# Padded feature rows loaded whole, and each group's score products put one step behind its one-hot products

## The chip, the cores and the metric

The kernel runs on one core of a Trainium2 chip. The metric is the device time of one execution in microseconds (us). Three runs of the kernel before took 2100.96, 2101.25 and 2093.63 us; the median is 2100.96 us.

TensorE (PE) multiplies, VectorE (DVE) and ScalarE (ACT) work element by element, GpSimd (POOL) prepares gathers by index and does a few small operations, and SyncE (SP) issues the plain transfers. Every engine works through its own list of instructions strictly in order; an instruction that waits holds up all that stand behind it on its engine.

## The reference, cut to what matters

The model is one layer: a convolution and a state-space branch, a cross-attention, and a layer of product-key experts (PEER). The change lies in the last part, which for 256 tokens, 8 heads and 16 experts per head computes

```
q = (h @ w_q).reshape(tokens, 8, 2, 64)
s = einsum("thsk,hsnk->thsn", q, sub_keys)      # 128 scores per half
s1, i1 = top_k(s[..., 0, :], 16);  s2, i2 = top_k(s[..., 1, :], 16)
top_s, pos = top_k(all 256 sums of s1 and s2, 16)
idx = i1[...] * 128 + i2[...]                   # of the 16 sums taken
g = softmax(top_s)
act = gelu(einsum("td,tkd->tk", h, u_tab[idx])) # 128 experts per token
out = einsum("tk,tkd->td", g * act, v_tab[idx])
```

`u_tab` and `v_tab` have 16,384 rows of 2048 numbers.

## The kernel before

The tokens are two tiles of 128, tile 0 and tile 1. The scores `h . u` are computed in two parts. Columns 768 to 2047 of each chosen row of `u_tab` are gathered, one row for each of the 128 tokens at a time: POOL issues the gather (L924, into one of five buffers `u`), and DVE forms the dot product with the token (L926, with `hnF`). I call one such pair a dot; there are 256, 128 for each tile. For columns 0 to 767, `dense` multiplies all 16,384 rows with all tokens on PE (`sy`, L972, with `hnT`) and stores the scores in the large tiles `WA` (tile 0) and `WB` (tile 1). Dots and dense products run beside each other.

Then comes the settling: out of the 16,384 dense scores of a token, the 128 wanted ones have to be picked. An index is two numbers of 0 to 127, and a one-hot row of each is made by a small product: `feats` holds five numbers per pick and token (the square of the index in two parts, the index, and two ones), `C` five constants, and their product `d` is 1 - (index - k)^2, which after a Relu is 1 at the index and 0 elsewhere. For a group of four tokens, `extract` makes the two one-hot tiles `E` and `H` in this way (four products `d` at L992 and a Relu on ACT at L994 for each), and at once multiplies the scores by `E` (`y`, L1000 for tile 0 and L1003 for tile 1). `pick` multiplies `H` by `y` on DVE (L1010) and adds up the columns on PE (`more`, L1012). I call the DVE product of `pick` an H product. `LAG` says how many groups later `pick` follows. Each tile has 32 groups.

When tile 0 is picked, `finish` adds the dots and the picked scores, applies the gelu and the gate (`ptc`, `cT`, L907 to L917), and while tile 1 is picked, the weights of tile 0 are spread out into `WA` again: `left` makes the one-hot tiles `dr` and `L` (L1019, L1028), and `build` scales one (`R`, DVE, L1035), multiplies the two on PE (`pw`, L1038) and copies the result (ACT, L1039). After the last dot tile 1 is finished and the last 4 groups of tile 0 and the 32 of tile 1 are built. Only then does the last stage run, a dense product with `v_tab` beside gathers of it (from 1556 us on).

Four things set the order. The list of DVE is written by hand: the program emits a dot, then as many steps of the settling as a pace gives (2.2 steps per dot, a step being a `yield` in `settle`), then the next dot. The lists of the other engines are set by a planner. The settling begins at dot 176 (`SETTLE_AT`). The features lie in `fe_dram` in device memory and are loaded by `load_feats` into memory that is free by then: tile 0's into `hnF`, once the dots of tile 0 are done, and tile 1's into `hnT`, once the dense products are done. `load_feats` first clears its 128 rows on POOL (L934), since the four groups of rows that SP loads (L937) have 20 rows each, 5 for each of four tokens, and are placed 32 rows apart.

Of the kernel before, what the change touches and what calls it, by code (L numbers as in the profile page):

```python
# [9 lines left out]
F32 = mybir.dt.float32  # L10
F32R = mybir.dt.float32r
BF16 = mybir.dt.bfloat16
I32 = mybir.dt.int32
U32 = mybir.dt.uint32
AF = mybir.ActivationFunctionType
# [5 lines left out]
P = 128  # L21
T = 256
NTT = T // P
# [15 lines left out]
NSLOT = PH * TOPK  # L39
# [25 lines left out]
SETTLE_RATE = 2.2  # L65
SETTLE_AT = 176
FEATS_AT = 150
LAG = (2, 1)
DELAY = 16
HOLD = 4  # L70
RAW_BUFS = 4
HI_BUFS = 3
LO_BUFS = 4
FEAT = 5
NROW = 4 * FEAT


@with_exitstack
def trunk(ctx, tc, a, out, dbg=None):
# [12 lines left out]
    ones = consts.tile([P, P], F32, name="ones")  # L92
# [25 lines left out]

    C = consts.tile([P, 4, 4, P], BF16, name="C")
    c_dram = dram.tile([FEAT, P], BF16, name="c_dram")  # L120
    fe_dram = [dram.tile([P, FEAT, 2 * NSLOT], BF16, name=f"fe_dram{tt}") for tt in range(NTT)]

    def load_consts(t, ones):
        ones = ones[:, :2 * NSLOT].bitcast(BF16)
        G.memset(ones, 1.0)
        for d in fe_dram:
            SY.dma_start(d[:, 3:].rearrange("p f x -> p (f x)"), ones)
        rows, one_less_sq = t[0:1, :FEAT * P // 2].bitcast(BF16), t[0:1, 3 * P:4 * P]
        k = iota[0:1, :P]
        G.memset(rows[:, :2 * P], -1.0)  # L130
        G.tensor_scalar(rows[:, 2 * P:3 * P], k, 2.0, None, op0=ALU.mult)
        G.tensor_mul(one_less_sq, k, k)
        G.tensor_scalar(one_less_sq, one_less_sq, -1.0, 1.0, op0=ALU.mult, op1=ALU.add)
        G.tensor_copy(rows[:, 3 * P:4 * P], one_less_sq)
        G.tensor_sub(rows[:, 4 * P:], one_less_sq, rows[:, 3 * P:4 * P])
        SY.dma_start(c_dram.rearrange("f k -> (f k)")[None, :], rows)
        G.memset(C, 0.0)
        for b in range(4):
            for i in range(4):
                p0 = 32 * b + FEAT * i  # L140
                SY.dma_start(C[p0:p0 + FEAT, b, i, :], c_dram)

    wbx = ctx.enter_context(ExitStack())
# [787 lines left out]
    fe_at = [x[:, :NQ * NSLOT // 4].bitcast(BF16).rearrange("p (j s k) -> p j s k", s=2, k=NSLOT) for x in room]  # L931

    def load_feats(tt):
        G.memset(fe_at[tt], 0.0)  # L934
        src = fe_dram[tt].rearrange("(b j i) f x -> b (i f) j x", b=4, i=4)
        for b in range(4):
            SY.dma_start(fe_at[tt][32 * b:32 * b + NROW].rearrange("f j s k -> f j (s k)"), src[b])  # L937

    coef = [consts.tile([P, NSLOT], F32, name=f"coef{tt}") for tt in range(NTT)]
    vidx = [consts.tile([P, NSLOT], I32, name=f"vidx{tt}") for tt in range(NTT)]  # L940
# [40 lines left out]
    def feats(route, g):  # L981
        return fe_at[route.tt][:, g % 8], C[:, g // 8]

    def extract(route, g):
        psq, lr_q = settling_pools
        f, cs = feats(route, g)
        spread = route.tt == 0 and g % 4 > 1
        one = []
        for s, nm in ((1, "E"), (0, "H")):
            d = psq.tile([P, 4, P], F32, name="d")  # L990
            for i in range(4):
                PE.matmul(d[:, i, :], cs[:, i, :], f[:, s, :], start=i == 0, stop=i == 3, skip_group_check=True)  # L992
            one.append(lr_q.tile([P, 4, P], F32, name=nm, tag="R" if spread and nm == "H" else nm))
            S.activation(one[-1], d, AF.Relu)  # L994
        E, H = one
        y = psq.tile([P, 4, P], F32, name="y", tag="dr" if spread else "y")
        for i in range(4):
            t = 4 * g + i
            if route.tt == 0:
                PE.matmul(y[:, i, :], W[0][:, t, :], E[:, i, :], start=i == 0, stop=i == 3, skip_group_check=True)  # L1000
            else:
                for h in range(2):
                    PE.matmul(y[64 * h:64 * h + 64, i, :], by_token[:, h, t, :], E[:, i, :], start=i == 0, stop=i == 3,  # L1003
                              skip_group_check=True)
        return H, y

    def pick(route, g, H, y):
        if g == 0:
            route.more = psu.tile([P, NSLOT], F32, name="more", bufs=1)
        V.tensor_mul(H, H, y)  # L1010
        for i in range(4):
            PE.matmul(route.more[i * NQ:(i + 1) * NQ, :], onecol[:, NQ - g:2 * NQ - g], H[:, i, :], start=g == 0,  # L1012
                      stop=g == NQ - 1)
# [55 lines left out]

    def settle():  # L1070
        groups = P // 4
        held = {}
        for tt in range(NTT):
            lefts = []
            lag = LAG[tt]
            for n in range(groups + lag):
                if n < groups and (tt, n) not in held:
                    held[tt, n] = extract(routes[tt], n)
                    yield
                if n >= lag:  # L1080
                    pick(routes[tt], n - lag, *held[tt, n - lag])
                    yield
                if tt:
                    if n > HOLD:
                        build(routes[0], n - HOLD - 1, *lefts.pop())
                    if n >= HOLD:
                        lefts.append(left(routes[0], n - HOLD))
                    yield
            if tt == 0:
                while tick[0] <= NSLOT:  # L1090
                    yield
                for n in range(2):
                    held[1, n] = extract(routes[1], n)
                yield from routes[0].finish()
            else:
                held_left.append(lefts.pop())
# [157 lines left out]
```

## Time and profile before

| | us |
|---|---|
| median of three runs | 2100.96 |
| profiled execution, its own time | 2093.88 |
| span of its profile | 2092.1 |
| dense products of `u_tab` end, settling starts on PE | 1293.6 |
| first H product of tile 0 starts on DVE | 1320.5 |
| `cT` of tile 0 on DVE | 1388.6 |
| last `y` of tile 1 starts on PE | 1493.1 |
| last dot starts on DVE | 1503.8 |
| last stage starts on ACT and PE | about 1556 |

PE is busy for 94% of the span, DVE for 80%, ACT for 48% and POOL for 38%. The stages follow each other, so what matters is what each stretch waits for; a busy share of the whole span says little of it.

### The profile page before, as it was taken

How to read it: one execution, taken by the hardware profiler on the slowest of the kernel's cores; microseconds unless marked ns; L12 is line 12 of the kernel's file. 1: busy time of each engine (PE TensorE's matmuls, PEld its weight loads, DVE VectorE, ACT ScalarE, POOL GpSimd, SP SyncE). 2: the span in 40 equal slices, each digit the busy share in tenths (PEclk: the TensorE clock that was granted, in tenths of full speed). 3: DMA queues.
4: the chain of work that ended last, by engine and by line, in shares of the span. 5: the costliest groups of instructions: out<-in, count | busy, mean ns of one | idle time of the engine just before them, and what ended most of it. 6: DMA issues, size and time to landing. Idle time of an engine off the chain costs nothing.

```text
span 2092.1 us, 33295 instructions
## 1 busy us (share of the span) xinstructions
PE 1969.4 (94%) x12359; PEld 1689.5 (81%) x12379; DVE 1683.7 (80%) x2757; ACT 998.4 (48%) x1586; POOL 786.6 (38%) x590
## 2 busy tenths in 40 slices
PE   7999999999999999899999998689899999999997
PEld 7888886786899888778888887567677888888886
DVE  6699998995756558999976663988868899899998
ACT  5776665445545444333333323356563444444444
POOL 1111111000000003444446753643217677677775
PEclk9999999999999999999999999899999999999999
DMA  7888788757854567989999996988629999999996
GB/s 233 198 239 210 194 224 224 219 193 216 286 182 159 178 194 278 306 304 332 328 368 398 398 394 220 330 273 265 189 106 317 359 337 339 341 340 341 338 335 231
DMA packets 201428, 570.99 MB, mean 273 GB/s; under 512 B 31266, under 2 KB 37779, under 8 KB 201138
## 3 DMA queue, kind: packets, MB, share of 16 engines
q1 hardware_dynamic: 134130, 306.69, 43.8%
q0 software_dynamic: 67136, 262.18, 37.5%
q8 instruction: 97, 1.59, 0.3%
q14 instruction: 65, 0.53, 0.1%
HBM read 556.34 MB, written 12.45 MB: 272 GB/s over the span
## 4 chain that ended last, share of the span: by engine, by line
PE 56%; DVE 18%; issue 10%; DMA 8%; POOL 6%; ACT 2%; SPq 0%; DVEq 0%; POOLq 0%; ACTq 0%
PE acc L1201 8%; PE acc L1202 8%; PE acc L1200 8%; DVE u L926 5%; POOL u L924 5%; PE mm L202 3%; PE mm L212 3%; PE mm L201 3%; PE mm L203 3%; PE mm L210 3%; PE mm L211 3%; PE pw L1038 3%; PE y L1003 2%; DMA w_lo<-in_w_kv_mem 2%; PE y L1000 2%
## 5 line engine op out<-in xcount | busy, mean ns | idle before, releaser
L926 DVE SCALAR_TENSOR_TENSOR u<-u,hnF 128x1280 f32<-128x1280 f32 x256 | 387.7, 1517 | 110.9 <-DMA u<-in_peer_u,uidx 109.9
L1165 POOL DMA_INDIRECT v<-in_peer_v,vidx x256 | 388.3, 1517 | 187.8 <-DVE accg L1167 82.1
L924 POOL DMA_INDIRECT u<-in_peer_u,uidx x256 | 303.1, 1184 | 316.3 <-DVE u L926 226.0
L972 PE MATMUL sy<-hnT,ut 128*128 128x256 f32 x1536 | 356.0, 384 | 14.1 <-ACT ut L968 14.1
L187 ACT CAST w_hi<-w_raw 128x1024 fp32r<-128x1024 f32 (+2 forms) x228 | 231.2, 1017 | 242.5 <-PE mm L203 114.6
L972 PEld LDWEIGHTS sy<-hnT,ut 128*128 128x128 f32 x1536 | 286.7, 192 | 54.8 <-ACT ut L968 19.4
L192 DVE TENSOR_TENSOR w_lo<-w_raw,w_hi 128x1024 fp32r<-128x1024 f32 (+2 forms) x192 | 226.4, 1181 | 110.3 <-ACT w_hi L187 110.1
L103 ACT CAST vh<-vr 128x1472 fp32r<-128x1472 f32 x128 | 183.1, 1431 | 258.6 <-PE acc L1201 257.1
L1201 PE MATMUL acc<-vh,wl 128*128 128x512 f32 (+1 forms) x768 | 295.9, 385 | 6.1 <-DVE wl L1191 6.1
L1202 PE MATMUL acc<-vl,wh 128*128 128x512 f32 (+1 forms) x768 | 293.9, 385 | 0.8 <-DVE vl L104 0.8
L212 PE MATMUL mm<-aT_hi,w_lo 128*128 128x256 f32 x960 | 273.1, 292 | 15.7 <-DVE w_lo L192 6.6
L210 PE MATMUL mm<-aT_hi,w_hi 128*128 128x256 f32 x960 | 277.9, 292 | 0.7 <-ACT w_hi L187 0.7
L1200 PE MATMUL acc<-vh,wh 128*128 128x512 f32 (+1 forms) x768 | 275.7, 383 | 2.4 <-ACT vh L103 2.4
L211 PE MATMUL mm<-aT_lo,w_hi 128*128 128x256 f32 x960 | 275.3, 289 | 0.0
L104 DVE TENSOR_TENSOR vl<-vr,vh 128x1472 fp32r<-128x1472 f32 x128 | 216.7, 1693 | 42.5 <-ACT vh L103 42.1
L1167 DVE SCALAR_TENSOR_TENSOR accg<-v,coef,accg 128x576 f32<-128x576 f32 x256 | 208.8, 816 | 11.1 <-DMA v<-in_peer_v,vidx 7.1
L212 PEld LDWEIGHTS mm<-aT_hi,w_lo 128*128 128x128 f32 x960 | 184.2, 195 | 22.4 <-DVE w_lo L192 8.0
L210 PEld LDWEIGHTS mm<-aT_hi,w_hi 128*128 128x128 f32 x960 | 186.7, 195 | 6.6 <-issue 3.7
L211 PEld LDWEIGHTS mm<-aT_lo,w_hi 128*128 128x128 f32 x960 | 187.0, 195 | 3.4 <-issue 2.0
L1201 PEld LDWEIGHTS acc<-vh,wl 128*128 128x128 f32 x768 | 144.8, 189 | 36.8 <-DVE wl L1191 6.6
L1200 PEld LDWEIGHTS acc<-vh,wh 128*128 128x128 f32 x768 | 144.6, 188 | 28.4 <-ACT vh L103 2.6
L1202 PEld LDWEIGHTS acc<-vl,wh 128*128 128x128 f32 x768 | 144.8, 189 | 22.9 <-DVE vl L104 1.2
(380 smaller groups left out, 3193.8 us busy)
## 6 DMA issues: line engine op xcount, KB each, us to landing
vr<-in_peer_v SPq DMA_DIRECT2D x128, 736.0 KB
raw<-in_peer_u SPq DMA_DIRECT2D x128, 384.0 KB
w_raw<-in_w_kv_mem SPq DMA_DIRECT2D x64, 512.0 KB
w_raw<-in_w_in SPq DMA_DIRECT2D x48, 512.0 KB
w_raw<-in_w_out SPq DMA_DIRECT2D x32, 512.0 KB
w_raw<-in_w_q_mem SPq DMA_DIRECT2D x32, 512.0 KB
w_raw<-in_w_o_mem SPq DMA_DIRECT2D x32, 512.0 KB
w_lo<-in_w_kv_mem POOLq DMA_DIRECT2D x24, 512.0 KB, 7.8
```

Of the source, the lines that this page charges most:

```text
L187: S.copy(hi, raw)
L192: V.tensor_sub(lo, raw, hi.bitcast(F32))
L210: PE.matmul(o, wh, ah, start=first and cb % 2 == 0, stop=False, skip_group_check=True)
L211: PE.matmul(o, wh, al, start=False, stop=False, skip_group_check=True)
L212: PE.matmul(o, wl, ah, start=False, stop=last and end, skip_group_check=True)
L924: G.indirect_dma_start(out=u, out_offset=None, in_=a["peer_u"].rearrange("e (q c) -> (e q) c", c=GU), in_offset=bass.IndirectOffsetOnAxis( ...
L926: V.scalar_tensor_tensor(u, u, 1.0, hnF[:, self.tt, :], op0=ALU.mult, op1=ALU.mult, accum_out=self.act[:, j:j + 1])
L972: PE.matmul(ps[:, b % 2, :], ut[:, k, :], hnT[:, k, :], start=k == 0 and b % 2 == 0, stop=k == KD - 1 and b % 2 == 1, skip_group_check=True)
L1165: G.indirect_dma_start(out=v, out_offset=None, in_=table, in_offset=bass.IndirectOffsetOnAxis(ap=vidx[tt][:, j:j + 1], axis=0))
L1200: PE.matmul(o, wh[:, tt, :], vh[:, cs_], start=b == 0, stop=False)
L1201: PE.matmul(o, wl[:, tt, :], vh[:, cs_], start=False, stop=False)
L1202: PE.matmul(o, wh[:, tt, :], vl[:, cs_], start=False, stop=b == NB - 1)
```

## The change

1. `fe_dram` has 8 rows per pick instead of 5 (`ROWS`). The three more are zeros, written once at the start of the kernel, beside the ones that are written there already: eight small transfers on SP (L129, L131 of the changed kernel) instead of two. The constants `C` are placed 8 rows apart instead of 5. `load_feats` then loads all 32 rows of each of its four groups, and the clearing on POOL is gone.
2. `extract` is split. `onehots` makes `E` and `H` of a group, and `select` makes `y`. `settle` calls `onehots` for group n and then `select` for group n - 1; `pick` comes one group later than before (`LAG` is (3, 2) instead of (2, 1)). In tile 1, `H` of every third group lies in a part of `hnT` that the features don't use (`spare_h`). The loop over the groups has one step more per tile, and `onehots` no longer has a step of its own.

```diff
-LAG = (2, 1)
+LAG = (3, 2)
...
-NROW = 4 * FEAT
+ROWS = 8
...
-    fe_dram = [dram.tile([P, FEAT, 2 * NSLOT], BF16, name=f"fe_dram{tt}") for tt in range(NTT)]
+    fe_dram = [dram.tile([P, ROWS, 2 * NSLOT], BF16, name=f"fe_dram{tt}") for tt in range(NTT)]
...
-        ones = ones[:, :2 * NSLOT].bitcast(BF16)
-        G.memset(ones, 1.0)
+        fill = ones.bitcast(BF16)
+        n1, n0 = 2 * (FEAT - 3) * NSLOT, 2 * NSLOT
+        G.memset(fill[:, :n1], 1.0)
+        G.memset(fill[:, n1:n1 + n0], 0.0)
         for d in fe_dram:
-            SY.dma_start(d[:, 3:].rearrange("p f x -> p (f x)"), ones)
+            SY.dma_start(d[:, 3:FEAT].rearrange("p f x -> p (f x)"), fill[:, :n1])
+            for r in range(FEAT, ROWS):
+                SY.dma_start(d[:, r], fill[:, n1:n1 + n0])
...
-                p0 = 32 * b + FEAT * i
+                p0 = 32 * b + ROWS * i
...
     def load_feats(tt):
-        G.memset(fe_at[tt], 0.0)
         src = fe_dram[tt].rearrange("(b j i) f x -> b (i f) j x", b=4, i=4)
         for b in range(4):
-            SY.dma_start(fe_at[tt][32 * b:32 * b + NROW].rearrange("f j s k -> f j (s k)"), src[b])
+            SY.dma_start(fe_at[tt][32 * b:32 * b + 32].rearrange("f j s k -> f j (s k)"), src[b])
...
-    def extract(route, g):
+    spare_h = hnT[:, 4:6, :].rearrange("p k (i s) -> p (k i) s", s=P)
+
+    def onehots(route, g):
         psq, lr_q = settling_pools
         f, cs = feats(route, g)
-        spread = route.tt == 0 and g % 4 > 1
         one = []
         for s, nm in ((1, "E"), (0, "H")):
             d = psq.tile([P, 4, P], F32, name="d")
             for i in range(4):
                 PE.matmul(d[:, i, :], cs[:, i, :], f[:, s, :], start=i == 0, stop=i == 3, skip_group_check=True)
-            one.append(lr_q.tile([P, 4, P], F32, name=nm, tag="R" if spread and nm == "H" else nm))
-            S.activation(one[-1], d, AF.Relu)
-        E, H = one
-        y = psq.tile([P, 4, P], F32, name="y", tag="dr" if spread else "y")
+            if nm == "E":
+                x = lr_q.tile([P, 4, P], F32, name="E")
+            elif route.tt and g % 3 == 2:
+                x = spare_h
+            else:
+                x = lr_q.tile([P, 4, P], F32, name="H", tag="R" if route.tt == 0 and g % 4 > 1 else "H")
+            S.activation(x, d, AF.Relu)
+            one.append(x)
+        return one
+
+    def select(route, g, E, H):
+        psq, lr_q = settling_pools
+        y = psq.tile([P, 4, P], F32, name="y", tag="dr" if route.tt == 0 and g % 4 > 1 else "y")
...
-                if n < groups and (tt, n) not in held:
-                    held[tt, n] = extract(routes[tt], n)
-                    yield
+                if n < groups and (tt, n) not in ones_at:
+                    ones_at[tt, n] = onehots(routes[tt], n)
+                if 0 < n <= groups:
+                    held[tt, n - 1] = select(routes[tt], n - 1, *ones_at.pop((tt, n - 1)))
+                yield
                 if n >= lag:
-                    pick(routes[tt], n - lag, *held[tt, n - lag])
+                    pick(routes[tt], n - lag, *held.pop((tt, n - lag)))
                     yield
...
                 for n in range(2):
-                    held[1, n] = extract(routes[1], n)
+                    ones_at[1, n] = onehots(routes[1], n)
```

How the lists move at three places. First, POOL's list from the dense stage to the end of the settling, before:

```order
L856 TENSOR_TENSOR WB<-WB 128x512 x2
L924 DMA u<-in_peer_u,uidx 128x1280 x59
L934 MEMSET hnF 128x2048
L924 DMA u<-in_peer_u,uidx 128x1280 x35
L934 MEMSET hnT 128x2048
L924 DMA u<-in_peer_u,uidx 128x1280 x88
```

and now:

```order
L860 TENSOR_TENSOR WB<-WB 128x512 x2
L928 DMA u<-in_peer_u,uidx 128x1280 x9
L860 TENSOR_TENSOR WB<-WB 128x512 x2
L928 DMA u<-in_peer_u,uidx 128x1280 x182
L1180 DMA v<-in_peer_v,vidx_8418 128x576 x128
```

The clearing of `hnF` and of `hnT` stood among the gathers, the second ahead of the last 88; now the last 182 gathers follow each other with nothing between them. The loads of the features (SP) stay at their places.

Second, PE and ACT in the middle of tile 0's groups (a row of `d` stands for the four of its tile; numbers tell the tiles apart), before:

```order
L992 MATMUL d_12257<-hnF_7777,C_76 128x128
L992 MATMUL d_12264<-hnF_7777,C_76 128x128
L1012 MATMUL more_11822<-H_12191,onecol_8420 32x128 x4
L1000 MATMUL y_12271<-E_12262,WA_8432 128x128 x4
L994 ACTIVATE E_12262<-d_12257 128x512
```

and now:

```order
L996 MATMUL d_12252<-hnF_7784,C_76 128x128
L996 MATMUL d_12259<-hnF_7784,C_76 128x128
L1025 MATMUL more_11844<-H_12156,onecol_8427 32x128 x4
L996 MATMUL d_12279<-hnF_7784,C_76 128x128
L1013 MATMUL y_12293<-E_12257,WA_8439 128x128 x4
L1003 ACTIVATE E_12257<-d_12252 128x512
```

`y` read an `E` whose `d` stood three steps ahead of it on PE, in the same group; now the `d` of the next group's `E` (`d_12279`) stands between as well.

Third, DVE from `cT` of tile 0 on, and at the end of the dots. Before:

```order
L914 TENSOR_TENSOR cT<-cT,gT 128x128
L926 SCALAR_TENSOR_TENSOR u,act<-u,hnF 128x1280
L1010 TENSOR_TENSOR H<-H,y 128x512
...
L1010 TENSOR_TENSOR H<-H,y 128x512
L926 SCALAR_TENSOR_TENSOR u,act<-u,hnF 128x1280
L1035 SCALAR_TENSOR_TENSOR R<-dr,cT 128x512
L926 SCALAR_TENSOR_TENSOR u,act<-u,hnF 128x1280 x3
L1035 SCALAR_TENSOR_TENSOR R<-dr,cT 128x512
L926 SCALAR_TENSOR_TENSOR u,act<-u,hnF 128x1280
L1035 SCALAR_TENSOR_TENSOR R<-dr,cT 128x512
L926 SCALAR_TENSOR_TENSOR u,act<-u,hnF 128x1280
L914 TENSOR_TENSOR cT<-cT,gT 128x128
```

and now:

```order
L918 TENSOR_TENSOR cT<-cT,gT 128x128
L930 SCALAR_TENSOR_TENSOR u,act<-u,hnF 128x1280 x3
L1023 TENSOR_TENSOR H<-H,y 128x512
...
L1023 TENSOR_TENSOR H<-H,y 128x512
L930 SCALAR_TENSOR_TENSOR u,act<-u,hnF 128x1280 x2
L1048 SCALAR_TENSOR_TENSOR R<-dr,cT 128x512
L918 TENSOR_TENSOR cT<-cT,gT 128x128
```

Three dots instead of one stand between `cT` of tile 0 and the first H product of tile 1, and two dots instead of six behind the last H product. Ahead of the first H product of tile 0 stand 179 dots instead of 178. On PE the second `ptc` of tile 0 now stands directly behind the first, where one `d` tile stood between, and `ptc` of tile 1 no longer stands behind two `dr` that wait for the last `R`.

More of the change, by code (lines that the diff above doesn't have):

```diff
@@ L1071, in settle @@
         groups = P // 4
-        held = {}
+        ones_at, held = {}, {}
         for tt in range(NTT):
@@ L1076, in settle @@
             for n in range(groups + lag):
-                if n < groups and (tt, n) not in held:
-                    held[tt, n] = extract(routes[tt], n)
-                    yield
+                if n < groups and (tt, n) not in ones_at:
[3 more added lines that the diff above has]
+                yield
                 if n >= lag:
-                    pick(routes[tt], n - lag, *held[tt, n - lag])
+                    pick(routes[tt], n - lag, *held.pop((tt, n - lag)))
                     yield
                 if tt:
-                    if n > HOLD:
+                    if HOLD < n <= groups:
                         build(routes[0], n - HOLD - 1, *lefts.pop())
-                    if n >= HOLD:
+                    if HOLD <= n <= groups:
                         lefts.append(left(routes[0], n - HOLD))
```

## Prediction

> **What bounds the kernel now.** I read the stretches around the settling first.
>
> ```profile
> core 0: us, PE busy (x) PEld busy (x) DVE busy (x) ACT busy (x) POOL busy (x), PEclk, DMA share, GB/s
> 1245.00:1265.00 20.00, 19.13 (x101) 16.49 (x100) 14.26 (x19) 5.78 (x10) 15.46 (x10) 1.00 1.02 405
> 1275.00:1293.60 18.60, 17.74 (x93) 15.35 (x92) 0.32 (x2) 4.32 (x8) 0.60 (x1) 1.00 0.09 28
> 1293.60:1305.00 11.40, 7.83 (x81) 6.63 (x79) 1.68 (x3) 6.09 (x12) 6.82 (x7) 1.00 0.79 239
> 1305.00:1321.20 16.20, 0.00 (x0) 0.00 (x0) 13.92 (x20) 0.00 (x0) 11.60 (x8) 0.60 0.93 339
> 1391.00:1494.20 103.20, 99.78 (x1201) 75.34 (x1215) 94.33 (x141) 61.75 (x111) 43.68 (x43) 0.95 0.84 265
> 1494.20:1505.40 11.20, 5.84 (x37) 3.02 (x36) 10.95 (x16) 4.81 (x9) 0.94 (x1) 0.88 0.45 148
> 1505.40:1556.00 50.60, 48.19 (x333) 40.83 (x338) 33.28 (x51) 28.53 (x53) 0.00 (x0) 0.92 0.09 27
> 1556.00:2092.00 536.00, 512.85 (x2304) 433.90 (x2304) 475.62 (x658) 242.26 (x406) 388.34 (x256) 0.99 0.92 329
> ```
>
> PE is the bound in nearly every stretch. The exception is 1305 to 1321.2, where it does nothing at all, and just before, from 1275 to 1293.6, DVE and the DMA engines (share 0.09) do nothing. The timeline joins the two holes (start, duration, what, and the idle time ahead of it with its releaser):
>
> ```profile
> 1264.50 1.50 POOL L924 DMA_INDIRECT u<-in_peer_u,uidx  x1 [0.31 <-issue]
> 1293.00 1.80 POOL L934 MEMSET hnT<- 128x2048 bf16 x1 [27.00 <-PE sy L972]
> 1273.81 1.49 DVE L926 SCALAR_TENSOR_TENSOR u<-u,hnF 128x1280 f32<-128x1280 f32 x1 [1.01 <-DMA u<-in_peer_u,uidx]
> 1300.58 1.49 DVE L926 SCALAR_TENSOR_TENSOR u<-u,hnF 128x1280 f32<-128x1280 f32 x1 [25.27 <-DMA u<-in_peer_u,uidx]
> 1319.10 1.49 DVE L926 SCALAR_TENSOR_TENSOR u<-u,hnF 128x1280 f32<-128x1280 f32 x1 [0.27 <-DMA u<-in_peer_u,uidx]
> 1320.52 0.68 DVE L1010 TENSOR_TENSOR H<-H,y 128x512 f32<-128x512 f32 x1
> 1321.25 0.65 PE L1012 MATMUL more<-H,onecol 128*32 128x128 f32 x8 [16.26 <-DVE H L1010]
> ```
>
> The clearing of `hnT` reaches the head of POOL's list at 1266.0 and waits 27.0 us, until the last dense product has read `hnT`. The gathers queue behind it, DVE has no rows for 25.27 us, and ten dots that stand ahead of the first H product in DVE's list are done only afterwards, from 1300.58 to 1320.5. PE, four groups ahead, waits 16.26 us for that product.
>
> **The change, term by term,** against the profiled execution (2093.88 us, span 2092.1).
>
> *Term 1, the stall.* With no clearing the gathers go on at 1266. Eleven dots now stand ahead of the first H product. Their pace is about 2.1 us: 19 records (two for each dot) in 20 us in the first row above, beside the loads of `raw`, and (1319.10 - 1300.58)/9 = 2.06 without them. The last dot in hand ends at 1275.3, so the eleven end at 1275.3 + 11 x 2.1 = 1298.4. PE needs the first H product only after the fourth `y`, which in the trace starts at 1301.36:
>
> ```profile
> 1301.36 1.16 PE L1000 MATMUL y<-E,WA 128*128 128x128 f32 x8 [0.52 <-ACT E L994]
> DMA to landing us min/median/max: 4.5/7.5/12.8
> ```
>
> That is 1302.5, some 4 us later, so the whole 16.26 us goes. With all five buffers at the slowest landing a dot takes 12.8/5 = 2.56 us and the eleven end at 1303.5: 1 us is left over. Bounds 15.2 to 16.3; I take 16.3. The dots advanced use DMA engines that stand still now, and the last loads of `raw` were issued by 1274, so the dense products don't wait longer.
>
> *Term 2, the cold start.* After the hole PE runs slowly:
>
> ```profile
> 1321.84 2.08 PE L1000 MATMUL y<-E,WA 128*128 128x128 f32 x8
> 1326.73 1.16 PE L1000 MATMUL y<-E,WA 128*128 128x128 f32 x8
> ```
>
> One `y` costs 0.92 us more, at a granted clock of 0.60 in the stretch before; with the small products around it I take 1.5, bounds 0.9 to 2. [...]
>
> *Term 3, E before y.* The steady pattern of tile 0, and the waits of PE from 1293.6 to 1383:
>
> ```profile
> 1328.86 1.16 PE L1000 MATMUL y<-E,WA 128*128 128x128 f32 x8 [0.17 <-ACT E L994]
> 1329.85 0.61 PE L992 MATMUL d<-hnF,C 128*128 128x128 bf16 x8
> 1330.39 0.43 PE L1012 MATMUL more<-H,onecol 128*32 128x128 f32 x8
> 1330.99 1.16 PE L1000 MATMUL y<-E,WA 128*128 128x128 f32 x8 [0.17 <-ACT E L994]
> PE y L1000 <- ACT E L994: 4.8, 19, 0.8
> ```
>
> A group takes 2.13 us, of which 0.17 is the Relu of its own `E`. With another group's `d` between, it goes: 4.8 us less the first wait (0.8), which stays. I take 4.0, bounds 2 to 4.8. What then limits? DVE:
>
> ```profile
> 1343.86 1.48 DVE L926 SCALAR_TENSOR_TENSOR u<-u,hnF 128x1280 f32<-128x1280 f32 x1
> 1345.27 0.68 DVE L1010 TENSOR_TENSOR H<-H,y 128x512 f32<-128x512 f32 x1
> 1345.87 1.48 DVE L926 SCALAR_TENSOR_TENSOR u<-u,hnF 128x1280 f32<-128x1280 f32 x1
> ```
>
> A dot holds it for 1.41 us and an H product for 0.60. Tile 0's 32 products with the 29 dots among them take 32 x 0.60 + 29 x 1.41 = 60.1 us, from 1298.4 to 1358.5. The next fence shows DVE idle for 5.31 us ahead of `cT` at 1388.6, after the products and a last dot, so they end near 1382 now. DVE comes some 23 us earlier, the three terms give PE 21.8, and they fit.
>
> *Term 4, from tile 0 to tile 1: a loss.*
>
> ```profile
> 1388.61 0.29 DVE L914 TENSOR_TENSOR cT<-cT,gT 128x128 f32<-128x128 f32 x1 [5.31 <-ACT cT L911]
> 1390.97 0.66 PE L1012 MATMUL more<-H,onecol 128*32 128x128 f32 x8 [1.45 <-DVE H L1010]
> 1391.56 1.98 PE L1003 MATMUL y<-E,WB 128*64 128x128 f32 x16
> ```
>
> Now `more` of tile 1 starts 2.4 us after `cT`. With three dots between, it is 0.3 + 3 x 1.41 + 0.6 = 5.1, and PE, strictly in order, has nothing ahead of that `more` but the second `ptc`; behind it stand the `y` and every `d` of tile 1. That is 2.8 us lost; bounds 1 to 5, since one group more is in flight; I take 3. The restart there is slow already (`y` 1.98 us) and stays so.
>
> *Term 5, tile 1.* PE is busy for 99.78 of 103.2 us from 1391 on; the same products remain. At most 3.4 can be gained, at least 0; I take 1.
>
> *Term 6, the last dots.*
>
> ```profile
> 1493.14 1.09 PE L1003 MATMUL y<-E,WB 128*64 128x128 f32 x16 [0.17 <-ACT E L994]
> 1503.81 1.48 DVE L926 SCALAR_TENSOR_TENSOR u<-u,hnF 128x1280 f32<-128x1280 f32 x1
> 1505.45 0.77 PE L909 MATMUL ptc<-ident,act 128*128 128x128 f32 x2 [0.92 <-DVE u L926]
> ```
>
> From the last `y` to `ptc` pass 12.3 us, in which DVE does six dots and three `R` (6 x 1.41 + 3 x 0.60 = 10.3) after its last H product. Two dots and one `R` are left (3.4), and `ptc` stands ahead of the `dr` that waits for the last `R`. PE's own work between (5.84 busy in the row 1494.2 to 1505.4, and the Relus that it waits for) takes about 8, so 4 us go; bounds 0 to 6.9. Behind `ptc` the 50.6 us of building and the 536 us of the last stage stand as they are and move as a block.
>
> *Term 7, the start.* Six more small writes stand in SP's list among the first weights.
>
> ```profile
> 30.59 0.89 SPq L127 DMA_DIRECT2D fe_dram<-ones  x2
> 35.51 0.30 POOL L130 MEMSET crow<- 1x256 bf16 x1 [8.33 <-DMA fe_dram<-ones]
> 45.00:50.00 5.00, 5.00 (x44) 5.00 (x43) 1.66 (x2) 2.10 (x2) 0.00 (x0) 1.00 0.73 211
> ```
>
> At 0.45 us each they hold SP for 2.7 us; POOL's `crow`, and the write of the constants that SP waits for, come as much later. PE is fully busy there, and three weight loads instead of two now stand ahead of that wait. Bounds 0 to 2.7 lost; I take 0.5.
>
> *Nothing* I give the fuller load of the features: 128 rows instead of 80, 0.5 MB, which for tile 1 is first read some 60 us after its issue; if that cover were gone it would cost under 2 us. The first clearing (of `hnF`) held POOL for less than 2 us and nothing waited.
>
> The sum: 16.3 + 1.5 + 4 - 3 + 1 + 4 - 0.5 = **23.3 us** less, 2070.6 us for an execution like the profiled one. The median of the runs shown lies 7.1 us above that execution, and I can't tell at which level the changed kernel's median will fall, 2070.6 or 2077.7; I put it at **2073**. The bounds of the terms added up as independent (about 5 us either way) and the two levels give 2064 to 2083 for this case.
>
> **The rivals.**
>
> *The advanced dots run slowly* (0.15). Dense loads and gathers shared 405 GB/s, and if the eleven dots took 3.3 us each they would end at 1311.6; PE would still wait 9 us, and the gain be 14: 2080 to 2087. Against it speaks that nothing else loads after the last `raw`.
>
> *Gathers shut out by dots* (0.03). On POOL the settling's gathers read:
>
> ```profile
> L924 POOL DMA_INDIRECT u<-in_peer_u,uidx x74 | 79.7, 1077 | 94.5 <-DVE u L926 89.9 <-issue 4.3 <-DVE H L1010 0.3
> ```
>
> If a gather could not be issued while a dot runs, one dot would cost 1.49 + 1.08 + 0.3 = 2.87 us, the eleven would end at 1306.9, and 4.4 us of term 1 would remain: 2075 to 2082. [...] The trace disagrees: dots follow each other every 2.01 us with an H product between (1343.86 and 1345.87).
>
> *Slower: features and spare H share `hnT`* (0.05). Every third group of tile 1 writes its `H` into the tile from which PE reads the features. If PE's next `d` had to wait for the H product in it, ten groups would each lose a wait. It decides from 23.3/10 = 2.3 us per wait; at a whole group's time, 101.6/29 = 3.5 us between the `y` at 1391.56 and 1493.14, it costs 35, and the time is 2105 to 2113. Against it: the `more` of that `H` waits for the same H product and stands ahead of those `d` on PE.
>
> *No change* (0.06). The gathers meet another wait up to 1293, and the second part gives back in term 4 what it gains in terms 3 and 6: 2092 to 2101. For it speaks only that the dots read `hnF` too, whose first half tile 0's features fill; but that load is issued near 1195.
>
> **How the numbers follow.** The forecast has 0.71, the rivals 0.15, 0.03, 0.05 and 0.06. A measurement of this kernel tells about 0.5% from no change. Against 2101, faster by over 0.5% means below 2090.5: the forecast, the locked gathers and most of the first rival, 0.87. Within 0.5%: 0.08. Slower: 0.05. The range, 2061 to 2088, holds the forecast and most of the slow dots.
>
> **What would show it.** In the changed profile no clearing stands on POOL and no wait of 25 us on DVE; DVE works between 1275 and 1293; the first H product starts near 1298 and PE's first `more` waits for nothing (term 1); few `y` of tile 0 wait for `E` and a group takes 1.96 us (term 3); a hole of some 5 us stands behind `cT`, which comes near 1366 (term 4); the last `y` starts near 1472 and `ptc` 8 us later (terms 5 and 6); the last stage keeps its 536 us. A first H product after 1303, or a PE wait for an H product among tile 1's features, would make me wrong.

## The result, and the profile after

The changed kernel took **2064.7 us** (median of four runs, 2061.8 to 2068.76) against 2098.55 us for the kernel before (four runs). The ratio is 0.9843, with a 95% interval of 0.9815 to 0.987, so about 33 us less. The prediction was 2073 us with a range of 2061 to 2088. The direction and the range held, and the median lies 8 us under the number. The profiled execution took 2064.74 us, with a span of 2063.0. One run each of two kernels below, 2630.97 and 2443.26 us at a mean granted clock of 0.69 and 0.75, was slow and is left out of their medians.

Both holes of the stage around 1300 us are gone. The stretches of the changed kernel (columns as in the prediction):

```profile
core 0: us, PE busy (x) PEld busy (x) DVE busy (x) ACT busy (x) POOL busy (x), PEclk, DMA share, GB/s
1245.00:1265.00 20.00, 19.13 (x103) 16.57 (x102) 13.50 (x18) 6.32 (x12) 15.12 (x9) 1.00 1.02 411
1275.00:1293.60 18.60, 17.74 (x94) 15.42 (x93) 13.06 (x17) 4.53 (x9) 12.35 (x9) 1.00 1.01 398
1293.60:1305.00 11.40, 10.32 (x75) 9.11 (x73) 2.70 (x6) 5.14 (x11) 3.29 (x3) 1.00 0.91 286
1305.00:1321.00 16.00, 15.26 (x194) 12.89 (x193) 15.51 (x23) 9.24 (x17) 6.56 (x7) 1.00 0.73 216
1360.00:1380.00 20.00, 13.50 (x167) 9.25 (x168) 14.46 (x22) 8.03 (x16) 9.27 (x9) 0.84 0.68 238
```

From 1275 to 1293.6 DVE worked for 0.32 us and now works for 13.06; the DMA share there goes from 0.09 to 1.01. From 1305 to 1321 PE goes from nothing to 15.26 of 16 us. One hole is left, in the stretch around `cT`.

To see where the time went, I read from each trace when a few landmarks start, and subtract. "Change" and "before" stand twice because both kernels were profiled a second time. All rows are us.

| stage | before | before, again | padding alone | split alone | change | change, again |
|---|---|---|---|---|---|---|
| start to the first `d` of the settling | 1293.6 | 1300.5 | 1302.5 | 1289.6 | 1301.3 | 1296.6 |
| to the first H product | 26.9 | 27.1 | 2.7 | 27.7 | 2.8 | 2.8 |
| to the last H product of tile 0 | 60.7 | 60.4 | 67.5 | 58.1 | 58.7 | 58.9 |
| to the first H product of tile 1 | 9.0 | 9.0 | 7.3 | 10.5 | 12.1 | 12.1 |
| to the last `y` | 103.7 | 103.5 | 103.7 | 103.8 | 103.6 | 104.1 |
| to `ptc` of tile 1 | 11.8 | 11.9 | 11.9 | 5.3 | 5.3 | 5.3 |
| to the last copy of `pw` | 50.0 | 49.9 | 50.7 | 47.8 | 47.8 | 50.3 |
| to the eighth cast `vh` of the last stage | 35.6 | 35.4 | 28.5 | 28.5 | 28.8 | 28.9 |
| to the end of the span | 500.7 | 500.7 | 502.9 | 502.9 | 502.6 | 502.6 |

With the means of the two profiles of each kernel, the change gives 25.9 us up to the last H product of tile 0, loses 3.1 ahead of tile 1, gives 6.5 after the last `y`, some 0.9 in the building, 6.7 on entering the last stage, and loses 1.9 at the very end and 1.9 ahead of the settling. That sums up to 33 us. The 0.9, the 6.7 and the two losses of 1.9 had no place in the prediction. The loss ahead of the settling is smaller than the difference between two profiles of one kernel (1293.6 and 1300.5 us).

**The stall is gone as forecast.** The timeline of the changed kernel at the places that the prediction quoted:

```profile
1285.91 2.24 POOL L928 DMA_INDIRECT u<-in_peer_u,uidx  x1 [2.19 <-DVE u L930]
1274.75 1.54 DVE L930 SCALAR_TENSOR_TENSOR u<-u,hnF 128x1280 f32<-128x1280 f32 x1 [1.09 <-DMA u<-in_peer_u,uidx]
1293.96 1.49 DVE L930 SCALAR_TENSOR_TENSOR u<-u,hnF 128x1280 f32<-128x1280 f32 x1
1304.09 0.69 DVE L1023 TENSOR_TENSOR H<-H,y 128x512 f32<-128x512 f32 x1 [8.63 <-ACT E L1003]
1309.68 0.42 PE L1025 MATMUL more<-H,onecol 128*32 128x128 f32 x8
1310.03 1.16 PE L1013 MATMUL y<-E,WA 128*128 128x128 f32 x8
```

POOL waits at most for DVE to free a buffer. The ten dots from 1274.75 to 1293.96 have a pace of (1293.96 - 1274.75)/9 = 2.13 us, against the 2.1 taken. DVE is done with them 8.6 us before the first H product can start, and PE's first `more` waits for nothing. The `y` behind it takes 1.16 us, where the first one behind the hole took 2.08.

**Ahead of the settling** PE waits for two loads of `raw`, first in the changed kernel and then in the kernel before:

```profile
1219.97 1.51 PE L969 MATMUL ut<-ident,raw 128*128 128x128 f32 x6 [6.32 <-DMA raw<-in_peer_u]
1222.52 1.51 PE L969 MATMUL ut<-ident,raw 128*128 128x128 f32 x6 [1.04 <-DMA raw<-in_peer_u]
```

```profile
1214.47 0.85 PE L966 MATMUL ut<-ident,raw 128*128 128x128 f32 x6 [0.20 <-DMA raw<-in_peer_u]
1217.03 0.84 PE L966 MATMUL ut<-ident,raw 128*128 128x128 f32 x6 [1.71 <-DMA raw<-in_peer_u]
```

**On entering the last stage** PE of the kernel before waits 6.14 us for `wl`, a small split that stands on DVE behind four products with gathered rows of `v_tab` (`accg`), which wait for those rows. Its PE and DVE:

```profile
1574.05 0.79 PE L1201 MATMUL acc<-vh,wl 128*128 128x512 f32 x1 [6.14 <-DVE wl L1191]
1563.98 0.82 DVE L1167 SCALAR_TENSOR_TENSOR accg<-v,coef,accg 128x576 f32<-128x576 f32 x1 [2.15 <-DMA v<-in_peer_v,vidx]
1568.04 0.82 DVE L1167 SCALAR_TENSOR_TENSOR accg<-v,coef,accg 128x576 f32<-128x576 f32 x1 [3.24 <-DMA v<-in_peer_v,vidx]
1572.10 1.69 DVE L104 TENSOR_TENSOR vl<-vr,vh 128x1472 fp32r<-128x1472 f32 x1
1573.70 0.28 DVE L1191 TENSOR_TENSOR wl<-WA,wh 128x128 fp32r<-128x128 f32 x1
```

In the changed kernel the third split `vl` stands behind one such product, not four:

```profile
1539.23 0.82 DVE L1182 SCALAR_TENSOR_TENSOR accg<-v,coef,accg 128x576 f32<-128x576 f32 x1 [1.56 <-DMA v<-in_peer_v,vidx]
1541.83 1.70 DVE L104 TENSOR_TENSOR vl<-vr,vh 128x1472 fp32r<-128x1472 f32 x1 [1.78 <-ACT vh L103]
1544.81 0.50 PE L1216 MATMUL acc<-vh,wl 128*128 128x512 f32 x1 [0.28 <-DVE wl L1206]
```

DVE's list is written by hand only up to the end of the settling; here the planner sets it, and it chose otherwise although no line of this stage was edited.

### The profile page after: what moved, and what is told of

Its sections match the earlier page's. It is cut to its first block, busy times and chain, and to the rows that moved or that the text cites. A ratio compares the mean times of both kernels' runs of the same rounds, so it can differ in the third digit from the quotient of the medians.

```text
span 2063.0 us, 33320 instructions
## 1 busy us (share of the span) xinstructions
PE 1961.4 (95%) x12361; PEld 1684.1 (82%) x12379; DVE 1683.5 (82%) x2757; ACT 998.2 (48%) x1586; POOL 777.7 (38%) x589
## 4 chain that ended last, share of the span: by engine, by line
PE 55%; DVE 15%; issue 11%; DMA 9%; POOL 7%; ACT 2%; SPq 0%; POOLq 0%; DVEq 0%; ACTq 0%
PE acc L1216 8%; PE acc L1217 8%; PE acc L1215 8%; POOL u L928 6%; DVE u L930 5%; PE mm L206 4%; PE mm L205 4%; PE mm L207 3%; PE mm L216 3%; PE mm L214 3%; PE mm L215 3%; PE pw L1051 3%; DMA w_lo<-in_w_kv_mem 2%; PE y L1016 1%; DMA xc<-in_mem 1%
## 5 line engine op out<-in xcount | busy, mean ns | idle before, releaser
L928 POOL DMA_INDIRECT u<-in_peer_u,uidx x256 | 295.8, 1156 | 330.2 <-DVE u L930 243.3
L975 PE MATMUL sy<-hnT,ut 128*128 128x256 f32 x1536 | 357.6, 385 | 15.4 <-ACT ut L971 15.4
```

Source lines behind the costliest of these rows:

```text
L928: G.indirect_dma_start(out=u, out_offset=None, in_=a["peer_u"].rearrange("e (q c) -> (e q) c", c=GU), in_offset=bass.IndirectOffsetOnAxis( ...
L975: PE.matmul(ps[:, b % 2, :], ut[:, k, :], hnT[:, k, :], start=k == 0 and b % 2 == 0, stop=k == KD - 1 and b % 2 == 1, skip_group_check=True)
```

## The experiments

### Each half alone, and both kernels again

The padding alone is the kernel before with the first half of the change (cut, as are the edits that follow):

```diff
...
-        G.memset(fe_at[tt], 0.0)
...
-            SY.dma_start(fe_at[tt][32 * b:32 * b + NROW]...
+            SY.dma_start(fe_at[tt][32 * b:32 * b + 32]...
...
```

`fe_dram` and `C` have 8 rows per pick as in the change; `extract` and `LAG` are those of the kernel before.

> The padded rows alone; the pairing of groups as in the kernel before. Theory: the clearing of hnT that stands before the gathers on POOL is the cause of both holes (DVE 25 us, PE 16 us), so the padding alone gives terms 1 and 2, 18 us, and no term 3, 4 or 6. Its list on DVE enters the last stage in the changed kernel's order (a split of the rows ahead of the second dot), not in that of the kernel before; if that order is what made the last stage start 7 us sooner in the profile of the change, 7 us more: 2098.6 - 25 = 2074 us, 2081 if the dense products lose 7 us again as in the profile of the change. Rival, the split of the steps carries the gain and the hole on PE only moves: 2090 to 2098 us.

It took 2079.35 us, ratio 0.9902 (0.9871 to 0.9933), 20 us less. The hole on PE is gone (26.9 us to 2.7 in the table), but tile 0 now takes 67.5 us instead of 60.7. Term 1 and 2 together are therefore (26.9 + 60.7) - (2.7 + 67.5) = 17.4 us; the prediction had 17.8.

The split alone is the changed kernel with the first half taken back:

```diff
...
+        G.memset(fe_at[tt], 0.0)
...
-            SY.dma_start(fe_at[tt][32 * b:32 * b + 32]...
+            SY.dma_start(fe_at[tt][32 * b:32 * b + NROW]...
...
```

> The split into one-hot tiles and score products alone, with the clearing on POOL and the 20-row loads kept. Theory: POOL waits some 27 us again, DVE idles some 25 us, PE 16 us; terms 3 to 6 give -3 + 6 to 9 and little of term 3, since DVE is then the bound of tile 0; with the order on entering the last stage (7 us, this list has it too) 2098.6 - 12 = 2087 us. If the entry order is worth nothing, 2094. Rival, the split hides the stall (one more group in flight): PE's hole shrinks to 12 us and the time falls under 2083.

It took 2085.98 us, ratio 0.995 (0.9928 to 0.9973), 6 to 15 us less. The profile is of the fastest of its eight runs, 2076.05 us, 10 us under the median. The stall is there in full, on POOL, DVE and PE:

```profile
1288.96 1.80 POOL L934 MEMSET hnT<- 128x2048 bf16 x1 [26.76 <-PE sy L972]
1297.05 1.49 DVE L926 SCALAR_TENSOR_TENSOR u<-u,hnF 128x1280 f32<-128x1280 f32 x1 [24.80 <-issue]
1318.07 0.66 PE L1022 MATMUL more<-H,onecol 128*32 128x128 f32 x8 [15.44 <-DVE H L1020]
```

So the split doesn't hide it: one more group in flight takes only 0.8 us off PE's 16.3 (15.44 instead of 16.26).

The two halves give 20 and 13 us by their medians, the whole 33. It looks as if they simply added up, and they don't. The 6.7 us on entering the last stage (less 1.9 at the end) are in each of the three, so they are counted twice in 20 + 13. Against that stands a gain that only both together have. Up to the last H product of tile 0 the padding gives 17.4 us, the split 87.6 - 85.8 = 1.8, and both 25.9, which is 6.7 us more than the sum. The two nearly cancel.

The kernel before and the changed one, profiled again:

> The kernel before, once more. If the order on DVE is what delays the start of the last stage, its third split of value rows (vl) again ends some 12 us after the cast that feeds it starts, behind four dots; if it is chance, the gap is under 6 us in this profile. The wait for raw near 1214 us is under 2.5 us if the 20-row loads keep it short. Time 2094 to 2101 us.

> The changed kernel, once more. In its first profile PE waited 6.3 + 1.0 us for a load of raw at 1214 to 1222 us, which the kernel before did for 0.2 + 1.7 us. If the fuller feature loads (128 rows instead of 80), issued just ahead of it, are the cause, a wait of 5 us or more stands there again, here and in the padded kernel, and in neither of the two with 20-row loads. If it is chance, it stands in some profiles of both kinds. Time 2062 to 2069 us.

They took 2098.04 us (ratio 0.9996) and 2065.25 us (0.9842, 0.9807 to 0.9877). The second profile of each has the same entry to the last stage as the first (35.4 and 28.9 us), so that is no chance. PE's wait for `raw` is 7.2 us in the changed kernel again. In the kernel before it is 4.7, where it was 1.9 in the first profile and under 2.5 was expected.

### The order on entering the last stage

First the kernel before, in which DVE's list for seven blocks of the last stage is written out in the changed kernel's order, and then the changed kernel with the order of the kernel before. The numbers are blocks; `v` is a product with a gathered row, `vl` the split of the value rows, and `w` the two splits `wl` of a block, one per tile (those of block 3 stand apart in the changed kernel):

```
before:  w0 vl0 w1 vl1 v v v v vl2 w2 v vl3 v w3 v v vl4 ...
change:  w0 vl0 w1 vl1 v vl2 v w2 v vl3 w3 v w3 v v vl4 ...
```

```diff
...
-    for b in range(NB):
...
+    entry.enter_context(tc.manual_schedule(engines={mybir.EngineType.DVE}))
+    for what in ENTRY.split():
...
+    entry.close()
+    for b in range(ENTRY_N, NB):
...
```

`ENTRY` is the written list of blocks 0 to 6, and `ENTRY_N` is 7.

> The kernel before, with nothing of the change, but with DVE's list for the first seven blocks of the last stage written out in the order that the changed kernel has there (one v product, a split, one v product, instead of four v products ahead of the third split). Theory, the order is what made the last stage start sooner: PE's wait of 6 us for wl goes, from the last copy of pw to the eighth cast vh 28.8 us instead of 35.5, time 2098.6 - 6.5 = 2092 us. Rival, the sooner start of the last stage comes from the work ahead of it: 35 us and 2098 stay.

2092.66 us, ratio 0.998 (0.9962 to 0.9998). The stage from the last copy of `pw` to the eighth cast takes 29.15 us instead of 35.5, and the waits of PE there are down to this:

```profile
1555.68 0.50 PE L1208 MATMUL acc<-vh,wh 128*128 128x512 f32 x1 [2.39 <-ACT vh L105]
1557.81 0.50 PE L1210 MATMUL acc<-vl,wh 128*128 128x512 f32 x1 [0.93 <-DVE vl L106]
```

The order alone is worth 6.4 us in this stage, with none of the change's own edits. The whole time falls by 5 us by the medians (from 2097.64, measured beside it); the interval allows 0.4 to 8.

> The changed kernel with that order written out as it stands in the kernel before (four v products ahead of the third split). Theory: 35.5 us instead of 28.8 from the last copy of pw to the eighth cast vh, time 2065 + 6.7 = 2071.5 us; what is then left of the gain, 27 us, is that of the change as described. Rival: stays at 2065.

2065.94 us, ratio 0.9863 (0.9825 to 0.99). The stage takes 33.0 us, 4.2 more than in the changed kernel and not 6.7: PE waits 3.17 us for `wl` and not 6.14. At the end of the span this kernel is 2.2 us shorter (21.96 us instead of 24.15 from the last cast `vh`), because the planner's order there changed as well: its last operations on ACT and DVE stand as in the kernel before. In all that is too little to tell from no difference, as the rival had it. The order explains the sooner start; its worth in the changed kernel is 4.2 us, not the full 6.7.

### The fuller load of the features

The wait for `raw` was over 7 us in every profile with 128 feature rows and under 5 in those with 80 so far. One thing more differs between the two sorts: the loads of tile 0's features do not quite stay at their places in SP's list. With 80 rows all four stand behind the 106th load of `raw`, with 128 rows the first of them stands ahead of it. No run separates this from the rows. From here on all kernels have DVE's order on entering the last stage written out, as the changed kernel has it unless said otherwise. To test the load, tile 0 got 20-row loads again (cleared on POOL, where nothing had waited), and tile 1 20-row loads with 12 rows of zeros loaded beside them:

```diff
...
+        if tt == 0:
+            G.memset(fe_at[tt], 0.0)
...
-            SY.dma_start(fe_at[tt][32 * b:32 * b + 32]..., src[b])
+            SY.dma_start(fe_at[tt][32 * b:32 * b + NROW]..., src[b])
+            if tt:
+                SY.dma_start(fe_at[tt][32 * b + NROW:32 * b + 32]..., none)
...
```

> The changed kernel with the features of tile 0 loaded as 20 rows again (cleared on POOL, where nothing waited for it), and those of tile 1 as 20 rows with 12 rows of zeros loaded beside them, so that POOL still clears nothing between the gathers; the order on entering the last stage written out as the changed kernel has it. Theory, the fuller load of tile 0 delays the load of raw behind it: PE's two waits at 1214 to 1222 us fall from 7.3 us to the 1 to 4.7 us of the kernels with 20-row loads, and the time to about 2065 - 4 = 2061 us. Rival, chance or the longer list of gathers on POOL: the waits stay above 6 us, 2065.

2064.44 us, ratio 0.9835 (0.9799 to 0.9871). PE waits 4.1 us for `raw`, some 3.4 less; but in tile 1 this profile loses 3.5 us, of which 2.20 are a wait of DVE for a late row behind `cT` (0.30 in the changed kernel), so nothing is gained in time.

Then the opposite, the changed kernel with tile 0's features loaded twice:

```diff
...
-            SY.dma_start(fe_at[tt][32 * b:32 * b + 32]..., src[b])
+            for _ in range(2 - tt):
+                SY.dma_start(fe_at[tt][32 * b:32 * b + 32]..., src[b])
...
```

> The changed kernel with each of the four feature loads of tile 0 issued twice (256 rows instead of 128; the second brings the same numbers), the order on entering the last stage as it has it. Waits of PE for raw near 1214 to 1222 us so far: 1.1 to 4.7 us with 80 rows (5 profiles), 7.2 to 7.8 us with 128 rows (5 profiles), so about 0.1 us per row. Theory, the rows moved set the wait: 15 to 20 us here, and the time 10 us longer than the changed kernel's, 2075 us. Rival, it is the place of one load ahead of a raw in SP's list and not the rows: 7 to 8 us again, 2065.

2079.1 us, ratio 0.9905 (0.9886 to 0.9924), 14 us slower than the changed kernel. The waits add up to 19.1 us, with a third one:

```profile
1222.81 1.51 PE L972 MATMUL ut<-ident,raw 128*128 128x128 f32 x6 [6.27 <-DMA raw<-in_peer_u]
1225.66 1.51 PE L972 MATMUL ut<-ident,raw 128*128 128x128 f32 x6 [1.34 <-DMA raw<-in_peer_u]
1245.85 1.51 PE L972 MATMUL ut<-ident,raw 128*128 128x128 f32 x6 [11.48 <-DMA raw<-in_peer_u]
```

The first two waits are what one load gives; the third comes with the second load. That one goes to the same place, so SP itself waits for the first copies to land, with loads of `raw` behind in its list (us in total, times, longest):

```profile
SPq L943 <- DMA hnF<-fe_dram: 10.9, 4, 3.5
```

The feature packets went on all that time, from 1197.8 to 1242.4 us by the packet records, so SP's wait left no pause in them. So the feature load does delay PE, and more of it delays more. But a last kernel, again with 20-row loads (and the third split ahead of the first row product on DVE), shows that with 80 rows PE can wait as long (against the kernel with 20-row loads):

```diff
...
-ENTRY = "w0 x0 v0 w1 x1 v1 g v2 g w2 x2 g v3 ..."
+ENTRY = "w0 x0 v0 w1 x1 v1 v2 g w2 x2 g v3 w3 g x3 ..."   # v: split vl, g: row product
...
```

> The kernel with 20-row loads and zero rows beside them (feats20), entering the last stage with the third split ahead of the first v product on DVE. Theory: PE's waits for raw 1 to 4.7 us as in feats20, from the last copy of pw to the eighth cast vh under 28.6 us, and the late row of 2.2 us on DVE behind cT, seen in feats20 alone, chance: 2058 to 2063 us. Rival: the zero rows loaded beside the features delay the first gathers of tile 1 and that wait comes back: 2064.

2063.28 us, ratio 0.9831 (0.9813 to 0.9848); the lowest median of all, and not to be told from the changed kernel's. The new order gains nothing: the entry takes 29.6 us, where under 28.6 was expected, and the late row behind `cT`, which had been put down to chance, is there again with 1.43 us. The profile is of the slowest of its six runs, 2075.01 us, and has this wait, with one of 1.05 us behind it:

```profile
1225.04 1.51 PE L977 MATMUL ut<-ident,raw 128*128 128x128 f32 x6 [6.32 <-DMA raw<-in_peer_u]
```

With 80 rows the waits of six profiles are thus 1.1, 1.9, 2.3, 4.1, 4.7 and 7.4 us, with 128 rows those of five are 7.2, 7.2, 7.4, 7.7 and 7.8. On the mean that is 3.6 against 7.5, some 4 us, and the settling starts at 1296.4 and 1300.7 us. By the packet records the 80 rows are under way for 11.8 to 12.5 us, from their first packet to their last, in the three profiles with waits under 2.5 us, and for 15.7 to 16.0 in the other three; the 128 rows take 20.5 to 21.8, with one load of `raw` among them. So the wait goes with the time that the features are under way; why this differs between loads of 80 rows is open.

### The dots ahead of tile 1

Term 4 said that three dots between `cT` and tile 1's first H product cost 2.8 us. Here the score product of tile 1's first group is made ahead of `finish`, and the loop over tile 1 starts two steps further on:

```diff
...
-            for n in range(groups + lag):
+            for n in range(2 * tt, groups + lag):
...
-                if 0 < n <= groups:
+                if 0 < n <= groups and (tt, n - 1) not in held:
...
+                held[1, 0] = select(routes[1], 0, *ones_at.pop((1, 0)))
                 yield from routes[0].finish()
...
```

> The changed kernel with the score product of tile 1's first group made ahead of finish, so that the loop over tile 1 starts two steps further on and two dots instead of three stand between cT and the first H product of tile 1 on DVE; the order on entering the last stage as the changed kernel has it. Theory, term 4 is those dots: cT to the first H product 3.0 us instead of 4.4, and 1.4 to 2.8 us less in all: 2062.5 to 2064. Rival, something else ends there (the second ptc, the y): no change, 2065.

2066.55 us, ratio 0.9856 (0.9823 to 0.989), no gain. The H product comes 3.03 us after `cT` instead of 4.44, as expected. But what doesn't stand there stands at the end, where four dots and not two follow the last H product: from the last `y` to `ptc` it takes 7.7 us instead of 5.3. The loss at this place is real, and moving the dots only moves it.

## Why the prediction was right, and where it was wrong

**Terms 1 and 2 (17.8 us): right, by cause and size.** The padding alone gives 17.4 for both; no run has the hole without the slow restart, so their shares are not measured apart. The cause is shown by the two halves: with the clearing, POOL waits 26.8 us and PE 15.4, whatever the order of the groups; without it both waits are gone. The eleven dots, due at 1298.4, were done at 1295.4 in the changed kernel. That profile left them room, since PE came 7.6 us later to the settling than in the first profile of before; in the second, where it came 3.0 us later, 4.9 us were left.

**Term 3 (4.0, bounds 2 to 4.8): the mechanism right, the size wrong; 8.6 us.** The step that failed is the price: the 4.8 us of waits for `E` that the trace of before lists are less than the Relu costs. That the hole stood beside them is not the reason, since PE's pace is 2.13 us per group with the hole and without it, and the list is no longer with the padding alone. Before (as in the prediction), and with the padding alone (us in total, times, longest):

```profile
PE y L1000 <- ACT E L994: 4.8, 19, 0.8
PE y L1003 <- ACT E L997: 4.3, 16, 0.8
```

What the hole hides is the pace itself: with four groups ready, DVE was the bound of tile 0 (60.7 us before, against the 60.1 worked out), and so the split alone gains only 1.8 us there. Without the hole, PE is the bound. The steady pattern with the padding alone, and then with the whole change:

```profile
1366.28 0.43 PE L1015 MATMUL more<-H,onecol 128*32 128x128 f32 x8
1366.87 1.16 PE L1003 MATMUL y<-E,WA 128*128 128x128 f32 x8 [0.17 <-ACT E L997]
1367.87 0.61 PE L995 MATMUL d<-hnF,C 128*128 128x128 bf16 x8
1368.41 0.43 PE L1015 MATMUL more<-H,onecol 128*32 128x128 f32 x8
```

```profile
1345.34 0.43 PE L1025 MATMUL more<-H,onecol 128*32 128x128 f32 x8
1345.69 1.16 PE L1013 MATMUL y<-E,WA 128*128 128x128 f32 x8
1346.69 0.61 PE L996 MATMUL d<-hnF,C 128*128 128x128 bf16 x8
1347.23 0.42 PE L1025 MATMUL more<-H,onecol 128*32 128x128 f32 x8
```

A group takes 2.13 us with the padding alone and 1.89 in the changed kernel. The wait is shown as 0.17, but `y` starts 0.59 us after `more` starts, and without the wait 0.35, so 0.24 us go in each of 32 groups, 7.7 us; the remaining 0.9 I have not traced. The prediction had PE's 2.13 us and DVE's 60.1/32 = 1.88 in front of it, which give 32 x 0.25 = 8 us; it took 0.17 for the whole of the Relu's cost (1.96 us per group, where 1.89 came) and priced the term by a sum of waits instead of by the pace. DVE's limit was right: 60.1 us for tile 0 were forecast, and from the first H product at 1304.09 to the end of the last dot at 1364.9 it took 60.8.

**Term 4 (-3): right.** `cT` to the first H product goes from 1.62 to 4.44 us, 2.8 lost:

```profile
1370.44 0.29 DVE L918 TENSOR_TENSOR cT<-cT,gT 128x128 f32<-128x128 f32 x1 [5.54 <-ACT cT L915]
1375.71 0.66 PE L1025 MATMUL more<-H,onecol 128*32 128x128 f32 x8 [4.60 <-DVE H L1023]
1376.30 1.98 PE L1016 MATMUL y<-E,WB 128*64 128x128 f32 x16
```

The hole of some 5 us behind `cT` is there (4.60), and the restart is slow, as said.

**Term 5 (+1, 0 to 3.4): nothing**, 103.6 and 104.1 us against 103.7 and 103.5.

**Term 6 (+4, 0 to 6.9): mis-sized, 6.5 us.** From the last `y` to `ptc`:

```profile
1477.67 1.09 PE L1016 MATMUL y<-E,WB 128*64 128x128 f32 x16
1481.31 1.49 DVE L930 SCALAR_TENSOR_TENSOR u<-u,hnF 128x1280 f32<-128x1280 f32 x1
1483.70 0.38 PE L913 MATMUL ptc<-ident,act 128*128 128x128 f32 x2
```

PE's own work there takes 6 us and not the "about 8" of the prediction, and `ptc` waits for no dot. (The table counts from the last product of that `y`: 5.3 us, where it was 11.8.) The split alone, which has only this part, shows the same 5.3 us.

**Term 7 (-0.5): not to be seen.** The first stages differ between two profiles of one kernel by more than that.

**"Nothing" for the fuller feature load: wrong, some 4 us.** The prediction asked who reads the features, and found 60 us of cover. What was late is the load of `raw` that stands behind them, and that has no cover. The number of rows was in the text; the question who else uses the queue was not.

**"Stand as they are and move as a block": wrong, 6.7 us gained and 1.9 lost.** The prediction treated the last stage as given, because no line of it was edited. Its order is the planner's, and the change, each half alone as well, made it choose another order than in the kernel before, here and at the very end. The kernel before with that order alone shows 6.4 us.

So of the 33 us, 23.3 were forecast by mechanism, the sizes of terms 3 and 6 gave some 7 us more, the planner's new order nearly 5, and the delayed `raw` took some of it back. The gain is thus some 10 us larger than the 23.3 of the sum, and the forecast lies only 8 us off since it was set between two levels. That it came out as near is in part luck: errors of both signs met.

**The rivals.** Slow dots: no, 2.13 us each. Gathers shut out by dots, at 2.87 us each: no, by the same number. But gathers are held up beside dots, and the prediction's "the trace disagrees" goes too far: it shows that the price is wrong, and not that nothing holds a gather up. Two gathers and the dots beside them in the kernel before:

```profile
1321.12 1.49 DVE L926 SCALAR_TENSOR_TENSOR u<-u,hnF 128x1280 f32<-128x1280 f32 x1
1321.71 1.71 POOL L924 DMA_INDIRECT u<-in_peer_u,uidx  x1 [0.30 <-issue]
1339.59 0.93 POOL L924 DMA_INDIRECT u<-in_peer_u,uidx  x1 [0.86 <-DVE u L926]
1339.84 1.48 DVE L926 SCALAR_TENSOR_TENSOR u<-u,hnF 128x1280 f32<-128x1280 f32 x1
```

The gather that starts 0.59 us into a dot takes 1.71 us and ends 0.81 us after the dot; the one that starts ahead of a dot takes 0.93 us, and the dot no longer than otherwise (1.48 us). In all twelve profiles every gather of `u` that starts over 0.05 us into a dot, 39 to 64 in each, ends 0.80 to 0.82 us after it. What holds it up, the rows don't show. Beside the H products it costs no time: the gather that is held up is for a later dot, and its 1.71 us and the 0.30 ahead of it fit into the 2.01 us of a dot with an H product. Features and spare H in one tile: PE's only waits on that account in tile 1 are 0.5 us for `hnT`, and tile 1 takes as long as before. No other wait took the place of the clearing.

## What to carry to other kernels

Price a removed wait by the pace of the steady pattern with and without it, not by the sum of the waits that the trace lists: here 0.17 us listed stood for 0.24 per group. A transfer that nobody waits for can still delay the one behind it on its queue (here PE waited 7.5 us for `raw` on the mean with 128 feature rows ahead of it, and 3.6 with 80), so ask for each added transfer what is issued next. Where a planner sets the order, a stage that no edit touches may change as well; compare its order before calling it unmoved, and time both halves of a change alone before saying which gave what, since halves that seem to add up may not.

## What was not expected of the hardware

**Small packets beside large ones.** Doubling the feature load moves 0.52 MB more and adds 11.6 us to PE's waits for `raw` (19.1 against 7.5), some 0.045 MB per us, in a stretch where the DMA engines otherwise move about 400 GB/s, or 0.4 MB per us. By the packet records, the features are 512-byte packets, 1024 of them for 128 rows, at 27 ns (median) each, and the gathers beside them 5120-byte packets at 200 ns. From 1230 to 1234 us of the kernel with the doubled load the records have 264 packets of the features, 17 of `raw` on the same queue, and 257 of the gathers: about as many of the features as of the gathers, for 0.14 MB against 1.3. In the changed kernel, while the features are under way (1205.6 to 1227.4 us), they are 1024, 509 and 1123. How an engine picks its next packet is not shown: the records don't tell which engine took which.

**When PE's clock drops.** The changed kernel enters the last stage with a wait of 2.39 us on PE, the kernel before as well, and the changed kernel with the old entry order has a wait of 3.17 us a little later. In this order, each with the row behind it:

```profile
1533.99 0.74 PE L1215 MATMUL acc<-vh,wh 128*128 128x512 f32 x1 [2.39 <-ACT vh L103]
1534.53 0.63 PE L1216 MATMUL acc<-vh,wl 128*128 128x512 f32 x1
```

```profile
1558.15 0.50 PE L1200 MATMUL acc<-vh,wh 128*128 128x512 f32 x1 [2.39 <-ACT vh L103]
1558.49 0.39 PE L1201 MATMUL acc<-vh,wl 128*128 128x512 f32 x1
```

```profile
1546.63 0.50 PE L1224 MATMUL acc<-vh,wl 128*128 128x512 f32 x1 [3.17 <-DVE wl L1209]
1546.96 0.40 PE L1225 MATMUL acc<-vl,wh 128*128 128x512 f32 x1
```

The same wait is followed by slow products once (0.63 us, granted clock 0.72 from 1532 to 1538) and by fast ones once (0.39, clock 1.00 from 1556 to 1562), and a longer one by fast ones (0.40, clock 1.00 from 1543 to 1549). The length of a wait alone doesn't decide it; what does, these rows don't show.
